# Tokens and first weights in one block, two more weight units fetched in the set-up, one power for sixteen columns

## The chip, the cores and the metric

The kernel runs on one core of a Trainium2 chip. The metric is the device time of one execution in microseconds (us). A core has TensorE (matrix products, with a weight load before each), VectorE, ScalarE, GpSimd and SyncE (SP), which here only issues DMAs. In the profile these are PE and PEld, DVE, ACT, POOL and SP; "SPq" is the issue of a DMA by SP, "ACTq" by ScalarE.

## What is computed

One layer of a decoder trunk on 512 tokens of 1024 channels, in float32. The change touches only its beginning:

```
h  = RMSNorm(x)                      # x: 512 x 1024
z  = h @ W_in                        # columns: retention q/k/v/gate, attention q/k/v of 3 groups, gates
aq = RMSNorm(aq per head); ak = RMSNorm(ak per head); rotary on both
x  = x + W_o( sig(g_A) * (retention @ W_A) + sig(g_B) * (attention @ W_B) )
x  = x + W_down( relu(RMSNorm(x) @ W_up)^2 )
x  = x + sig(RMSNorm(x) @ W_pg) * (p @ W_pp)
```

The attention has three groups of four heads of 128 channels. Each head's q and k are normed over their 128 channels.

## The kernel before

**Precision and tiling.** Each float32 product is made of three matmuls on parts: `hi` (rounded) and `lo` (the rest) of both operands, hi*hi, hi*lo, lo*hi (`mm3`, lines 249 to 251). Weights come from memory in units of 256 rows by 512 columns (`raw`, 512 KB, six buffers), and a unit is split into `whi` and `wlo` (`split_unit`, four buffers each): ScalarE writes `whi` (line 237), VectorE writes `wlo` (line 238). A panel of 512 output columns has 1024 rows, so four units. The plan's first three panels are the first group's queries (units 0 to 3), keys (4 to 7) and values (8 to 11).

**Order.** In the first group's query and key projections ScalarE and VectorE run in the order in which the program writes their instructions; the other queues are ordered by the planner, by readiness and place in the program. A queue runs its instructions one behind another, and one that waits holds what is behind it. `ahead(n)` splits units ahead of their use; `fetch(n)` issues the loads of the first n units of the plan, and a load waits for a free `raw` buffer.

**Set-up (`setup`).** ScalarE issues the gain columns (line 382). Then SP issues, for each of eight blocks of 128 rows, that block of the transposed `x` (line 388, from an array `x_cols`, 128 x 512) and that of the first panel's weights (line 391, from `w_in`, whose rows are 9728 long). Of the first weight block the first 64 rows are issued by ScalarE (line 393) and the rest by SP (line 394). Then come tables (lines 428, 432), `fetch(6)` (units 4 and 5, line 200) and the four tiles of `x` in rows (line 402). Seven matmuls on a constant run meanwhile (line 411).

**First panel (`first_panel`).** For each row block k, ScalarE and VectorE split `x` times the gain into `hh` and `hl` (lines 449, 450) and the weights into `whi` and `wlo`; the very first `whi` is a cast on VectorE (line 233). TensorE runs block 0 (lines 468 to 472), then blocks 1 to 3 for all four token tiles, then blocks 4 to 7 tile by tile, and hands each finished tile t to `consume` (line 586). That squares the four heads with a sum per head (ScalarE, line 591) and rotates the tile (VectorE, lines 544 to 549).

**The norms of the first panel.** The query projection of the first group is `lazy`: the factors of the token norm are not known until ScalarE has squared the four `x` tiles (`token_squares`, line 517) at the end of the panel. `token_factors` then makes them, with one power on GpSimd (line 527). Behind it, for each of the four tiles, `factor` makes a small VectorE instruction (line 613) and a power of 128x4 on GpSimd (line 614), and `scale` multiplies the rotated tile (VectorE, line 618). In VectorE's order the `wlo` of the key panel's units 6 and 7 follow the four scalings.

Of the kernel before, what the change touches and what calls it, by code (L numbers as in the profile page):

```python
# [11 lines left out]
F32 = mybir.dt.float32  # L12
F32R = mybir.dt.float32r
AF = mybir.ActivationFunctionType
ALU = mybir.AluOpType
AX = mybir.AxisListType

P = 128
S = 512
D = 1024  # L20
NT = S // P
KD = D // P
DFF = 4 * D
NF = DFF // 512
H = 4
HD = 128
# [9 lines left out]
AQ, AK, AV = 3072, 4608, 6144  # L36
# [40 lines left out]
class Block:  # L77
# [299 lines left out]
    def setup(self):  # L377
        nc, a = self.nc, self.a
        self.gcol = self.const.tile([P, 48], F32, name="gcol")
        xr = [self.big("xr") for _ in range(2)]  # L380
        self.x_cols = [xr[k // 4][:, k % 4] for k in range(KD)]
        nc.scalar.dma_start(self.gcol, a["vec_cols"])
        for u in range(KD // 2):
            src, _ = self.plan[u]
            raw = self.wraw.tile([P, 1024], F32, tag="raw", name=self.nm("raw")).rearrange("p (k n) -> p k n", k=2)
            for k in range(2):
                c = slice((2 * u + k) * P, (2 * u + k + 1) * P)
                nc.sync.dma_start(self.x_cols[2 * u + k], a["x_cols"][c])
                w = src[k * P : (k + 1) * P]
                if u or k:  # L390
                    nc.sync.dma_start(raw[:, k], w)
                else:
                    nc.scalar.dma_start(raw[: P // 2, k], w[: P // 2])
                    nc.sync.dma_start(raw[P // 2 :, k], w[P // 2 :])
            self.raws.append((raw, None))
        self.load_tables()
        self.fetch(6)
        self.x_tiles = []
        xb = [self.big("x") for _ in range(2)]
        for t in range(NT):  # L400
            v = xb[t // 2].rearrange("p (t c) n -> p t (c n)", t=2)[:, t % 2]
            nc.sync.dma_start(v, a["x"][0, t * P : (t + 1) * P])
            self.x_tiles.append(v)
        self.ident = self.const.tile([P, P], F32, name="ident")
        make_identity(nc, self.ident)
        warm = self.tmp("warm")
        nc.vector.memset(warm, 0.0)
        nc.scalar.activation(warm[:, 500:501], warm[:, 501:502], AF.Copy)
        wb, wps = warm.bitcast(mybir.dt.bfloat16), self.bank("warm")
        for _ in range(WARM):  # L410
            nc.tensor.matmul(wps, wb[:, :P], wb[:, :512], start=True, stop=True)
        self.mhalf = self.const.tile([P, H], F32, name="mhalf")
        nc.gpsimd.memset(self.mhalf, -0.5)
# [166 lines left out]
    def att_proj(self, g, n):  # L580
        nc = self.nc
        lazy = g == 0 and n == 0
        tabs = [] if lazy else [self.ready_tabs if g == 0 else self.tables(g, n)]
        rots, sums = [], []

        def consume(t, ps):
            ss, v, r = self.small(H, "ss"), self.small(H, "v"), self.small(H, "r")
            j = self.tmp("j")
            for h in range(H):
                c = slice(h * HD, (h + 1) * HD)  # L590
                nc.scalar.activation(j[:, c], ps[:, c], AF.Square, accum_out=ss[:, h : h + 1])
            C, Sn = tabs[0]
            rots.append(self.rotate(ps, C[:, t], Sn[:, t]))
            sums.append((ss, v, r))
            if not lazy:
                factor(t)
                if t:
                    scale(t - 1)
                if t == NT - 1:
                    scale(t)  # L600
            elif t == NT - 2:
                self.token_squares(0)
            elif t == NT - 1:
                self.token_squares(2)
                self.token_factors()
                for i in range(NT):
                    factor(i)
                for i in range(NT):
                    scale(i)

        def factor(t):
            ss, v, r = sums[t]
            nc.vector.tensor_scalar(v, ss, 1.0 / HD, self.floor[:, t : t + 1], op0=ALU.mult, op1=ALU.add)
            nc.gpsimd.tensor_tensor(r, v, self.mhalf[:, :H], op=ALU.pow)

        def scale(t):
            o = rots[t].rearrange("p (h e) -> p h e", h=H)
            nc.vector.tensor_tensor(o, o, sums[t][2].unsqueeze(2).to_broadcast([P, H, HD]), op=ALU.mult)

        if lazy:  # L620
            self.first_panel(consume, lambda: tabs.append(self.tables(g, n)))
        else:
            self.rows_gemm(self.hT, KD, consume)
        return self.heads_T(rots, g > 0, 16 if lazy else 12)
# [601 lines left out]
```

## Time and profile before

| | |
|---|---|
| median of 3 runs | 996.74 us (996.7 to 998.17) |
| the profiled execution | 997.21 us, its span 995.4 us |
| TensorE busy | 984.7 us, 4588 matmuls |
| VectorE busy | 647.6 us |
| ScalarE busy | 461.8 us |
| GpSimd busy | 97.4 us |
| moved by DMA | 141.15 MB, 142 GB/s on the mean |

The span runs from the first to the last instruction of the program in the profiled execution; its time is somewhat longer than the span. Times in the views below are counted from the span's start. A busy TensorE is one that has a matmul in its pipeline.

### The profile page before, as it was taken

The page shows a single profiled execution, that of the slowest core. Times are in us where ns is not written, and L with a number is a line of the kernel's source. Part 1 is how long each engine was busy: PE and PEld are TensorE (multiplying, and loading weights), DVE is VectorE, ACT ScalarE, POOL GpSimd, SP SyncE. Part 2 cuts the span into 40 slices and gives each one's busy share as a digit, 9 for nine tenths or more (in the row PEclk, how much of TensorE's full clock was granted, in tenths as well). Part 3 has the DMA queues.
Part 4 walks back from the last instruction along what each step waited for, and adds up shares of the span by engine and source line. Part 5 has one row for each costly group of instructions (what it writes and reads, how often), then busy time and mean ns, then how long its engine had stood idle before and what let it go on. Part 6 is the DMA issues. An engine that isn't in the chain of part 4 may idle for free.

```text
span 995.4 us, 12449 instructions
## 1 busy us (share of the span) xinstructions
PE 984.7 (99%) x4588; PEld 826.1 (83%) x4588; DVE 647.6 (65%) x1014; ACT 461.8 (46%) x938; POOL 97.4 (10%) x98
## 2 busy tenths in 40 slices
PE   8999999999999999999999999999999999999998
PEld 6788899889887888888888878888888888888886
DVE  6866675774878344554643696668667759766953
ACT  5535344433433334342422447764564565465451
POOL 0210220220000010001002010110101001000000
PEclk9999999999999999999999999999999999999999
DMA  9632132323353312222346496758659766875911
GB/s 337 240 101 76 54 106 85 105 76 106 93 142 120 113 43 85 86 85 85 132 146 166 125 233 193 190 128 225 179 136 212 203 167 153 238 160 131 312 54 53
DMA packets 90781, 141.15 MB, mean 142 GB/s; under 512 B 6320, under 2 KB 40416, under 8 KB 90720
## 3 DMA queue, kind: packets, MB, share of 16 engines
q1 hardware_dynamic: 79616, 119.22, 37.5%
q0 software_dynamic: 10880, 20.97, 12.7%
q8 instruction: 36, 0.59, 0.2%
q10 hardware_dynamic: 224, 0.16, 0.1%
q14 instruction: 25, 0.20, 0.1%
HBM read 136.10 MB, written 4.24 MB: 141 GB/s over the span
## 4 chain that ended last, share of the span: by engine, by line
PE 94%; DVE 4%; issue 1%; DMA 0%; ACT 0%; POOL 0%; ACTq 0%; DVEq 0%; POOLq 0%
PE pg L251 25%; PE pg L250 25%; PE pg L249 25%; PE pb L251 3%; PE pb L249 3%; PE pb L250 3%; PE po L700 1%; PE ph L559 1%; PE pt L325 1%; PE sc L677 1%; DVE wlo L238 1%; PE ry L899 1%; PE pe L651 1%; PE kv L887 1%; PE sc L683 1%
## 5 line engine op out<-in xcount | busy, mean ns | idle before, releaser
L238 DVE TENSOR_TENSOR wlo<-raw,whi 128x1024 fp32r<-128x1024 f32 (+1 forms) x166 | 196.8, 1191 | 103.8 <-ACT whi L237 101.8
L237 ACT ACTIVATE whi<-raw 128x1024 fp32r<-128x1024 f32 (+1 forms) x165 | 169.5, 1032 | 195.3 <-PE pg L251 75.4
L249 PE MATMUL pg<-whi,hh 128*128 128x512 f32 x444 | 178.6, 402 | 0.0
L250 PE MATMUL pg<-wlo,hh 128*128 128x512 f32 x444 | 173.6, 391 | 1.0 <-DVE wlo L238 1.0
L251 PE MATMUL pg<-whi,hl 128*128 128x512 f32 x444 | 173.7, 391 | 0.0
L250 PEld LDWEIGHTS pg<-wlo,hh 128*128 128x128 f32 x444 | 91.4, 206 | 15.3 <-DVE wlo L238 1.4
L251 PEld LDWEIGHTS pg<-whi,hl 128*128 128x128 f32 x444 | 91.1, 205 | 15.1
L249 PEld LDWEIGHTS pg<-whi,hh 128*128 128x128 f32 x444 | 91.3, 206 | 14.0
L249 PE MATMUL pg<-h2h,whi 128*128 128x512 f32 x256 | 99.6, 389 | 0.0
L250 PE MATMUL pg<-h2l,whi 128*128 128x512 f32 x256 | 99.6, 389 | 0.0
L251 PE MATMUL pg<-h2h,wlo 128*128 128x512 f32 x256 | 99.6, 389 | 0.0
L242 ACT ACTIVATE whi<-raw,gcol 128x256 fp32r<-128x256 f32 (+1 forms) x144 | 66.1, 523 | 21.3 <-PE pg L250 12.4
L243 DVE SCALAR_TENSOR_TENSOR wlo<-raw,gcol,whi 128x256 fp32r<-128x256 f32 (+1 forms) x144 | 65.5, 510 | 15.6 <-ACT whi L242 15.6
L202 POOL DMA_DIRECT2D raw<-in_w_down x32 | 38.6, 1206 | 302.4 <-DMA raw<-in_w_down 147.8
L249 PE MATMUL pg<-hh,whi 128*128 128x512 f32 x160 | 64.0, 400 | 0.0
L249 PE MATMUL pg<-whi,uh 128*128 128x512 f32 x160 | 62.8, 392 | 0.0
L251 PE MATMUL pg<-whi,ul 128*128 128x512 f32 x160 | 62.6, 392 | 0.0
L250 PE MATMUL pg<-wlo,uh 128*128 128x512 f32 x160 | 62.4, 390 | 0.0
L251 PE MATMUL pg<-hh,wlo 128*128 128x512 f32 x160 | 62.4, 390 | 0.0
L250 PE MATMUL pg<-hl,whi 128*128 128x512 f32 x160 | 62.3, 390 | 0.0
L250 PEld LDWEIGHTS pg<-h2l,whi 128*128 128x128 f32 x256 | 48.0, 188 | 10.0
L251 PEld LDWEIGHTS pg<-h2h,wlo 128*128 128x128 f32 x256 | 48.0, 188 | 10.0
(201 smaller groups left out, 1685.2 us busy)
## 6 DMA issues: line engine op xcount, KB each, us to landing
raw<-in_w_in SPq DMA_DIRECT2D x72, 512.0 KB, 4.1
raw<-in_w_down SPq DMA_DIRECT2D x48, 512.0 KB, 4.3
raw<-in_w_up SPq DMA_DIRECT2D x32, 512.0 KB, 5.2
raw<-in_w_down POOLq DMA_DIRECT2D x32, 512.0 KB, 6.7
raw<-in_w_o SPq DMA_DIRECT2D x12, 512.0 KB, 4.3
x<-in_x SPq DMA_DIRECT2D x8, 512.0 KB, 7.1
raw<-in_w_ret_out SPq DMA_DIRECT2D x8, 512.0 KB, 3.5
raw<-in_w_o POOLq DMA_DIRECT2D x8, 512.0 KB, 5.8
```

The costliest lines, as they stand in the source:

```text
L202: self.nc.gpsimd.dma_start(raw, rows(add[0]), accum_op=ALU.add)
L237: self.pin(nc.scalar.activation(R(hi[:, i]), raw[:, i], AF.Copy))
L238: nc.vector.tensor_tensor(R(lo[:, i]), raw[:, i], hi[:, i], op=ALU.subtract)
L242: self.pin(nc.scalar.activation(R(hi[:, i]), raw[:, i], AF.Copy, scale=g))
L243: nc.vector.scalar_tensor_tensor(R(lo[:, i]), raw[:, i], g, hi[:, i], op0=ALU.mult, op1=ALU.subtract)
L249: t.matmul(ps, sh, mh, start=first, stop=False, skip_group_check=more)
L250: t.matmul(ps, sh, ml, start=False, stop=False, skip_group_check=more)
L251: t.matmul(ps, sl, mh, start=False, stop=last, skip_group_check=more)
L325: nc.tensor.transpose(ps[:, k * P : (k + 1) * P], part[:, k * P : (k + 1) * P], self.ident)
L559: self.nc.tensor.transpose(ps[:, t * P : (t + 1) * P], rots[t][:, h * HD : (h + 1) * HD], self.ident)
L651: self.nc.tensor.transpose(ps[:, k * P : (k + 1) * P], e[:, k * P : (k + 1) * P], self.ident)
L677: nc.tensor.matmul(sc[:, h * P : (h + 1) * P], qT[:, h, rs], kT[:, h, rs], start=True, stop=True)
```

## The change

The transposed `x` and the first panel's weights are laid side by side on the host in one array `front` of 1024 x 1024: row r has the 512 tokens of channel r and then the 512 weights of row r. Each block of 128 rows is loaded by one DMA of 512 KB from SP, except block 0, whose `x` and weights are loaded by one DMA each; ScalarE issues none of them. The blocks lie in four of the 16 `big` buffers (two before), and the first panel takes no `raw` buffer. `fetch(8)` takes the place of `fetch(6)`, so that units 6 and 7 are issued before the `x` tiles. In the lazy projection the four powers of 128x4 become one of 128x16: the four small VectorE instructions write four columns each of one tile, one power reads all of it, and the four scalings follow.

```diff
@@ setup
         self.gcol = self.const.tile([P, 48], F32, name="gcol")
-        xr = [self.big("xr") for _ in range(2)]
-        self.x_cols = [xr[k // 4][:, k % 4] for k in range(KD)]
         nc.scalar.dma_start(self.gcol, a["vec_cols"])
+        self.x_cols = []
         for u in range(KD // 2):
-            src, _ = self.plan[u]
-            raw = self.wraw.tile([P, 1024], F32, tag="raw", name=self.nm("raw")).rearrange("p (k n) -> p k n", k=2)
+            front = self.big("front")
             for k in range(2):
-                c = slice((2 * u + k) * P, (2 * u + k + 1) * P)
-                nc.sync.dma_start(self.x_cols[2 * u + k], a["x_cols"][c])
-                w = src[k * P : (k + 1) * P]
-                if u or k:
-                    nc.sync.dma_start(raw[:, k], w)
-                else:
-                    nc.scalar.dma_start(raw[: P // 2, k], w[: P // 2])
-                    nc.sync.dma_start(raw[P // 2 :, k], w[P // 2 :])
-            self.raws.append((raw, None))
+                both = front[:, 2 * k : 2 * k + 2]
+                src = a["front"][(2 * u + k) * P : (2 * u + k + 1) * P].rearrange("p (c n) -> p c n", c=2)
+                for c in (0, 1) if u == 0 and k == 0 else (slice(0, 2),):
+                    nc.sync.dma_start(both[:, c], src[:, c])
+                self.x_cols.append(both[:, 0])
+            self.raws.append((front.rearrange("p (k c) n -> p k c n", c=2)[:, :, 1], None))
         self.load_tables()
-        self.fetch(6)
+        self.fetch(8)
@@ att_proj, consume
                 self.token_factors()
+                v4, r4 = self.small(NT * H, "v"), self.small(NT * H, "r")
                 for i in range(NT):
-                    factor(i)
+                    c = slice(i * H, (i + 1) * H)
+                    nc.vector.tensor_scalar(v4[:, c], sums[i][0], 1.0 / HD, self.floor[:, i : i + 1], op0=ALU.mult, op1=ALU.add)
+                    sums[i] = None, None, r4[:, c]
+                nc.gpsimd.tensor_tensor(r4, v4, self.mhalf.unsqueeze(1).to_broadcast([P, NT, H]), op=ALU.pow)
                 for i in range(NT):
                     scale(i)
@@ kernel
-    data["x_cols"] = np.ascontiguousarray(inputs["x"][0].T)
+    data["front"] = np.ascontiguousarray(np.concatenate(
+        [inputs["x"][0].T, inputs["w_in"][0][:, AQ : AQ + 512]], 1))
```

## Rows read from the trace of the kernel before

**Rows 1.** The page's first part: busy us, share of the span, instructions.

```profile
PE 984.7 (99%) x4588; PEld 826.1 (83%) x4588; DVE 647.6 (65%) x1014; ACT 461.8 (46%) x938; POOL 97.4 (10%) x98
```

**Rows 2.** Waits of TensorE over the span: us in total, times, longest.

```profile
PE pg L468 <- DVE whi L233: 1.9, 1, 1.9
...
PE ph L559 <- DVE ro L549: 1.2, 1, 1.2
PE pg L250 <- DVE wlo L238: 1.0, 1, 1.0
PE pc L756 <- DVE cw L754: 0.8, 1, 0.8
```

**Rows 3.** Timeline of the first 10 us: start, duration, engine, line, what [idle before].

```profile
1.18 0.55 SPq L394 DMA_DIRECT2D raw<-in_w_in  x1
...
3.96 0.72 ACT L449 ACTIVATE hh<-xr,gcol 128x512 fp32r<-128x512 f32 x1 [0.69 <-DMA gcol<-in_vec_cols]
...
5.96 0.43 DVE L233 CAST whi<-raw 128x512 fp32r<-128x512 f32 x1 [4.56 <-DMA raw<-in_w_in]
...
6.44 0.72 ACT L449 ACTIVATE hh<-xr,gcol 128x512 fp32r<-128x512 f32 x1 [1.76 <-DMA xr<-in_x_cols]
...
6.53 1.17 PE L468 MATMUL pg<-whi,hh 128*128 128x512 f32 x4 [1.90 <-DVE whi L233]
...
8.23 0.68 DVE L238 TENSOR_TENSOR wlo<-raw,whi 128x512 fp32r<-128x512 f32 x1
...
9.58 0.39 PE L250 MATMUL pg<-wlo,hh 128*128 128x512 f32 x1
```

**Rows 4.** DMA issues of the first 3 us: KB each, median us to landing.

```profile
raw<-in_w_in SPq DMA_DIRECT2D x1, 256.0 KB, 4.7
raw<-in_w_in SPq DMA_DIRECT2D x1, 128.0 KB, 3.1
```

**Rows 5.** Windows: length, busy by engine, granted clock, DMA share, GB/s.

```profile
6.50:9.40 2.90, 2.87 (x13) 2.41 (x14) 2.90 (x5) 2.52 (x5) 0.00 (x0) 1.00 1.03 372
```

**Rows 6.** Timeline: issue of the `x` tiles, and ScalarE's first and last square.

```profile
13.40 2.38 SPq L402 DMA_DIRECT2D x<-in_x  x4
...
27.25 1.11 ACT L517 ACTIVATE j<-x 128x1024 f32<-128x1024 f32 x1
...
31.72 1.06 ACT L517 ACTIVATE j<-x 128x1024 f32<-128x1024 f32 x1
```

**Rows 7.** The tile `x` in the first 40 us: its DMAs' landing.

```profile
DMA to landing us min/median/max: 8.3/9.2/11.1
```

**Rows 8.** The tile `raw` in the first 40 us: split times, waits for its DMAs.

```profile
L237 ACT ACTIVATE whi<-raw x15: 632/643/1061, 7.1 to 39.5; 128x512 fp32r<-128x512 f32 x11, 128x1024 fp32r<-128x1024 f32 x4
...
  DMA raw<-in_w_in: 4.6, 1
```

**Rows 9.** GpSimd's groups by shape: busy us, mean ns, idle before.

```profile
L614 POOL TENSOR_TENSOR r<-v,mhalf 128x4 f32<-128x4 f32 x24 | 29.9, 1251 | 156.4 <-DVE v L613 153.5 <-ACT whi L237 2.9
L315 POOL TENSOR_TENSOR r<-v,mhalf 128x1 f32<-128x1 f32 x16 | 8.7, 542 | 202.7 <-DVE v L314 202.7
L950 POOL TENSOR_TENSOR gm<-gt,gt 128x512 f32<-128x512 f32 x4 | 6.5, 1636 | 35.3 <-DVE gt L942 31.1 <-issue 4.2
```

**Rows 10.** Timelines of GpSimd, VectorE and TensorE from 34 to 41 us.

```profile
34.81 3.94 POOL L614 TENSOR_TENSOR r<-v,mhalf 128x4 f32<-128x4 f32 x4
...
35.86 0.69 DVE L618 TENSOR_TENSOR ro<-ro,r 128x512 f32<-128x512 f32 x1 [1.17 <-POOL r L614]
...
38.78 0.69 DVE L618 TENSOR_TENSOR ro<-ro,r 128x512 f32<-128x512 f32 x1 [0.28 <-POOL r L614]
39.39 4.62 DVE L238 TENSOR_TENSOR wlo<-raw,whi 128x1024 fp32r<-128x1024 f32 x4
...
39.27 0.39 PE L249 MATMUL pg<-whi,hh 128*128 128x512 f32 x1
40.66 0.50 PE L250 MATMUL pg<-wlo,hh 128*128 128x512 f32 x1 [1.00 <-DVE wlo L238]
```

## Prediction

> **What bounds the kernel now.** I read the page's first part before anything else: TensorE is busy for 984.7 of 995.4 us [rows 1]. Nothing in this change touches the number of its matmuls, so all that can be won or lost lies in the 10.7 us in which it is not busy. The list of TensorE's waits says where these are [rows 2]: 1.9 us before the first real matmul (line 468), 1.0 us at line 250 and two later ones of 1.2 and 0.8 us. The reader is to see that the list is short, and that two of its entries lie where the diff works.
>
> The first entry is opened by the timeline of the first 10 us [rows 3] with the landing times [rows 4]. The first weights' cast on VectorE waits 4.56 us for a DMA and starts at 5.96; the matmul follows at 6.53. The half of these weights that SP issued landed 3.1 us after its issue at 1.18, so at 4.3; what the cast waited for was the half on ScalarE's queue, at about 5.93. ScalarE had its own first input, the gain columns, at 3.96 and was through with `hh` at 4.7.
>
> The other entry lies at 39 us [rows 10]. The matmul at 39.27 is followed by the next at 40.66; the pace of this kernel is 0.22 us (13 matmuls in 2.87 us, [rows 5]), so 1.16 us are lost. It waits for `wlo` of the third weight unit of the key panel, and that stands on VectorE behind four scalings (line 618), each of which waits for its own power on GpSimd.
>
> **The block of memory (head).** Seventeen issues for eight row blocks become nine: `x` and weights of row block 0 by themselves on SP, then one of 512 KB for each later block. The bytes are the same, and the queue is full either way (372 GB/s from 6.5 to 9.4, [rows 5]), so fewer issues as such cost and save nothing; the DMA work hides them. The splits read views of the block with the same 128x512 shapes and cost what they cost. Four of the 16 big buffers are held where two were, until the panel's last split; no tile of this stretch needs the seventeenth. What moves is the first weights' second half: from ScalarE's queue to SP's, directly behind the first. 128 KB at 372 GB/s are 0.35 us, so the whole lands at 4.3 + 0.35 = 4.67 instead of 5.93. Bounds: 4.3 (as the first half now) and 5.93 (as now). From landing to first matmul it is 6.53 - 5.93 = 0.60 us; the new start is 5.27, or 1.26 us earlier.
>
> The next need is row block 1. Today its `x` lands by 6.44 (ScalarE's second `hh` starts then, released by it, [rows 3]) and its weights at 2.40 + 4.7 = 7.1 [rows 4]; with one transfer for both, `hh` must wait for the weights too. Call its landing T. Then `hh` takes 0.72, `whi` 0.64 [rows 8] and `wlo` 0.68 [rows 3]: the block's second matmul can go at T + 2.05. It goes at 9.58 today; with TensorE alone as the limit it would go at 5.27 + 3.05 = 8.32 (3.05 is today's distance from 6.53 to 9.58). For T I have two ends: 4.67 plus 512 KB at the full rate, 1.41 us, is 6.1; the weights' landing of today is 7.1. I take 6.5, nearer the low end, since 128 KB no longer compete from a second queue. That gives 8.55, a gain of **1.0 us**. T = 7.1 gives 9.15 and 0.45 us; first weights at 4.3 with T = 6.1 gives 8.15 and 1.4 us.
>
> A rule of the Trainium skill gives another figure: the page "DMA: Bandwidth & Descriptors" (section "Anatomy of one DMA — SWDGE (gpsimd) path") fits a DMA as about 2.0 us fixed plus its bytes at 436 GB/s, for GpSimd's path. By it, as an estimate, the first weights would land at 3.9, block 1 at 5.2, and the gain would be 1.8 us, so that the whole change came to nothing. The trace has 3.1 us for the landing of a half that the rule would put at 2.5 or so, so I stay with the rows.
>
> **Key weights ahead (`fetch(8)`).** Two more 512 KB loads stand on SP's queue ahead of the four `x` tiles. Who gains: nobody. In the first 40 us only one wait of an engine for weights is recorded, the 4.6 us at the start [rows 8]; the splits of the third and fourth key unit are held by the order of ScalarE and VectorE, not by their data. Who could lose: the `x` tiles, which come 1 MB later, 2.8 us at 372 GB/s. They are issued from 13.40 to 15.8 and land 8.3 to 11.1 us later, the first at 21.7, the last at about 26.6 [rows 6, 7]; behind the two loads that becomes 24.5 and 29.4. ScalarE squares the first at 27.25 and the last at 31.72 [rows 6]; with a head 1.0 us earlier that is 26.25 and 30.7. A margin of 1.3 us or more is left: cost 0 here. What is queued behind these squares, if the margin were gone, is the chain of the next part, so that a late tile costs its lateness in full.
>
> **One power for four tiles.** Removed: four powers of 128x4, 3.94 us together, 0.985 us each when they run one behind another. Added: one of 128x16. The trace has no such width. Nearest rows [rows 9]: a power of 128x1 takes 0.54 us, one of 128x4 1.25 us on the mean over the run (1.0 in this series). From one to four columns it grows, by 0.15 (to 1.0) to 0.24 us a column (to 1.25). So 16 columns take 0.54 + 15 x 0.15 = 2.8 at the least and 0.54 + 15 x 0.24 = 4.1 at the most by these, and 16/4 x 0.985 = 3.94 by the series itself. Costs of start that four instructions pay once each are already hidden in the series. I take 3.94, the row of the same place.
>
> What hangs on it is not GpSimd but the order behind it. Today the first scaling starts at 35.86, 1.05 us after the first power, and the other three run while later powers are worked; the last starts at 38.78 and `wlo` at 39.39 [rows 10], so a scaling costs VectorE 0.61 us. With one power no scaling can start before all 16 columns are there: 34.81 + 3.94 + 0.04 = 38.79. Four scalings, 2.44 us, put `wlo` at 41.23. That is **1.84 us later** than today. In general the shift is the power's duration less 2.10 us: 0.7 at 2.8 us, 2.0 at 4.1. TensorE is already waiting there, so the shift adds to its wait in full: 1.16 becomes 3.0 us. The four small VectorE instructions on the way (line 613) stay four, so nothing comes off there.
>
> **Sum.** Span 995.4 - 1.0 + 0 + 1.84 = 996.2. What follows is tied to TensorE's progress and moves with it: the later waits of 1.2 and 0.8 us are of VectorE's work on tiles that TensorE has just made. The profiled execution took 997.21 us, 1.81 around its span, so the same execution would take 998.0. It stood 0.47 us above the median of the three runs (996.74), so the median should be 997.5 us, 0.08% slower. Differences under 0.2% (2 us) can't be told from no change here, so this counts as the same.
>
> **Rivals.**
> *A power costs the same at any small width.* GpSimd's addition of 128x512 takes 1636 ns [rows 9], 3.2 ns a column; at such a price 16 columns take what 4 take, about 1.0 us. Then the scalings run from 35.86 on, `wlo` starts at 38.3, is done at 39.5, and the wait of 1.16 us is gone: 996.74 - 1.16 - 1.0 = 994.6. Against it stands the growth from one column to four. The page "GPSIMD Engine Reference" of the Trainium skill (section "Performance versus the Vector engine") has about 2.6 cycles an element for a two-input operation, which would lead here; the power's rows do not follow it. Chance 0.08.
> *The pair comes late.* If block 1 lands at 7.5 or the first weights at 5.9, the head gives nothing, and the median is 996.74 + 1.84 = 998.6, still within 0.2%. For it: the first transfers ran slowly (landings 3.1 us after 1.18, 4.7 us after 2.40). Against: the bytes ahead of both only become fewer. Chance 0.13.
> *The `x` tiles come late (slower).* They are now behind four weight units. Each us past 26.25 for the first, or 30.7 for the last, delays the squares, the powers and line 250 by one. It decides when the stall exceeds 1.2 us, the last tile landing after 31.9: with 1.5 us of stall the median would be 999.0. The 11.1 us of the slowest landing shows that a transfer can slip by 1 to 2 us, the margin is 1.3. Chance 0.07.
>
> **Chances and range.** My forecast has 0.70, the rivals 0.28, and 0.02 stays for anything else. Within the forecast the gain of 0.45 to 1.4 against the loss of 0.7 to 2.0 gives 996.0 to 998.3. The range of 8 in 10 takes in the late pair and part of the late tiles: 995.8 to 999.0. Faster by over 0.2% (below 994.75) needs the cheap power and the head's gain: 0.06. Slower by over 0.2% (above 998.73) needs late tiles, or a late pair with a power above 4.1 us: 0.10. The same: 0.84.
>
> **What the profile after would show.** The first real matmul near 5.3 and the second one of block 1 near 8.5. One power at line 606 or so of about 3.9 us, four scalings behind it without idle time between them, and a wait of TensorE at line 250 of 2.9 us where it was 1.0. No wait of ScalarE for `x`. A power near 1 us would make the forecast wrong towards faster, a recorded wait of ScalarE on `x` towards slower, and a first matmul still at 6.5 would shift it by one us.

## The result, and the profile after

The changed kernel takes 1001.52 us (median of 16 runs, 999.33 to 1003.45) against 998.25 us of the kernel before, timed beside it (16 runs, 996.47 to 1000.57): a ratio of 1.0031, 95% interval 1.0024 to 1.0039. That is slower, by 3.1 us; forecast were 0.8 us and no difference that can be told. The three runs shown ahead of the prediction (median 996.74) were at the lower end of the kernel's spread, for which the last experiments suggest a reason; put on that median, the ratio gives 999.8 us, which is outside the stated range too.

The profiled execution of the changed kernel has a span of 999.5 us, 4.1 more than before. The page's first part, beside [rows 1]:

```profile
PE 987.8 (99%) x4588; PEld 828.7 (83%) x4588; DVE 647.3 (65%) x1014; ACT 461.5 (46%) x938; POOL 96.4 (10%) x95
```

TensorE is busy for 3.1 us more, with as many matmuls, and not busy for 1.0 us more (11.7 where it was 10.7). So most of this loss does not lie in waits. TensorE's waits, beside [rows 2] (line 463 is 468 of before, 554 is 559, 755 is 756):

```profile
PE pg L250 <- DVE wlo L238: 2.5, 1, 2.5
...
PE ph L554 <- DVE ro L544: 1.2, 1, 1.2
PE pc L755 <- DVE cw L753: 1.0, 1, 1.0
PE pg L463 <- DVE whi L233: 0.8, 1, 0.8
```

The wait for the first weights shrank from 1.9 to 0.8 us; the one at line 250 grew from 1.0 to 2.5. What came of the first, in the timeline of the first 11 us, beside [rows 3] and, here first, two more matmul rows of before:

```profile
7.54 1.07 PE L470 MATMUL pg<-whi,hl 128*128 128x512 f32 x4
8.45 1.07 PE L472 MATMUL pg<-wlo,hh 128*128 128x512 f32 x4
```

And of the changed kernel:

```profile
4.81 0.43 DVE L233 CAST whi<-front 128x512 fp32r<-128x512 f32 x1 [3.41 <-DMA front<-in_front]
...
7.49 0.72 ACT L444 ACTIVATE hh<-front,gcol 128x512 fp32r<-128x512 f32 x1 [2.86 <-DMA front<-in_front]
...
5.38 2.05 PE L463 MATMUL pg<-whi,hh 128*128 128x512 f32 x4 [0.75 <-DVE whi L233]
7.23 1.91 PE L465 MATMUL pg<-whi,hl 128*128 128x512 f32 x4
8.94 1.16 PE L467 MATMUL pg<-wlo,hh 128*128 128x512 f32 x4
9.93 0.39 PE L249 MATMUL pg<-whi,hh 128*128 128x512 f32 x1
10.15 0.39 PE L250 MATMUL pg<-wlo,hh 128*128 128x512 f32 x1
```

TensorE starts at 5.38, as forecast (5.27), and still reaches the second matmul of row block 1 at 10.15 instead of 9.58. What took the gain here is the pace of the matmuls. The eight of lines 463 and 465 take 3.56 us (5.38 to 8.94), where the kernel before needed 1.92 (6.53 to 8.45): 0.43 us for each of line 465 and not 0.23, so they ran at the lower of TensorE's two clock levels (1.2 GHz).

The pair of block 1 landed only by 7.49 (I had 6.5), but in this execution that cost nothing: TensorE has no wait between 5.38 and 10.15. Where the clock is up early the late pair does hold it, as in the profile of e2 (the block alone, below), whose pair landed by 7.66:

```profile
7.66 0.72 ACT L444 ACTIVATE hh<-front,gcol 128x512 fp32r<-128x512 f32 x1 [3.12 <-DMA front<-in_front]
8.29 0.61 ACT L237 ACTIVATE whi<-front 128x512 fp32r<-128x512 f32 x1
...
7.21 1.07 PE L467 MATMUL pg<-wlo,hh 128*128 128x512 f32 x4
8.96 0.50 PE L249 MATMUL pg<-whi,hh 128*128 128x512 f32 x1 [0.68 <-ACT whi L237]
9.83 0.50 PE L250 MATMUL pg<-wlo,hh 128*128 128x512 f32 x1 [0.37 <-DVE wlo L238]
```

Either of the two is enough to undo the earlier start.

The stretch before line 250, by queue, beside [rows 10]:

```profile
33.26 0.69 DVE L568 TENSOR_TENSOR C<-rotc,mg 128x512 f32<-128x512 f32 x1 [0.61 <-DMA mg<-in_rot_gains]
...
36.09 2.90 POOL L606 TENSOR_TENSOR r<-v,mhalf 128x16 f32<-128x16 f32 x1
...
39.03 2.50 DVE L617 TENSOR_TENSOR ro<-ro,r 128x512 f32<-128x512 f32 x4 [3.07 <-POOL r L606]
41.45 4.62 DVE L238 TENSOR_TENSOR wlo<-raw,whi 128x1024 fp32r<-128x1024 f32 x4
...
39.85 0.39 PE L249 MATMUL pg<-whi,hh 128*128 128x512 f32 x1
42.72 0.50 PE L250 MATMUL pg<-wlo,hh 128*128 128x512 f32 x1 [2.48 <-DVE wlo L238]
```

The power takes 2.90 us and the four scalings follow it without idle time, as forecast in kind. New is the first row: VectorE waits for a DMA of `rot_gains`, the gains of the other groups' tables, which nothing in the diff names. And behind the gap, in windows (length; busy time of TensorE, its weight loads, VectorE, ScalarE and GpSimd; granted clock, DMA share, GB/s):

```profile
43.30:46.50 3.20, 3.20 (x9) 2.49 (x8) 2.77 (x3) 0.00 (x0) 0.00 (x0) 0.50 0.00 0
46.70:50.00 3.30, 3.30 (x16) 2.73 (x15) 1.67 (x4) 1.22 (x9) 0.00 (x0) 1.00 0.65 212
```

The granted clock is at half in the first window: 9 matmuls are started in its 3.2 us, 16 in the 3.3 us of the second. TensorE had just stood still for 2.5 us. Seven matmuls at 0.23 us are 1.6 us lost while TensorE counts as busy.

So the 4.1 us of this pair of profiles are: head +0.57; the late gains +0.7 (VectorE's chain is later by 1.28 at the first power, 36.09 - 34.81, of which 0.57 are the head); the power +0.8 (2.90 less 2.10, the prediction's own formula); the fall of the clock +1.6. About 0.4 is left, half of it at line 755, whose cause was not followed up.

### The profile page after: what moved, and what is told of

The parts are those of the page before. It is cut to its first block, busy times and chain, and to the rows that moved or that the text cites. A ratio compares the mean times of both kernels' runs of the same rounds, so it can differ in the third digit from the quotient of the medians.

```text
span 999.5 us, 12422 instructions
## 1 busy us (share of the span) xinstructions
PE 987.8 (99%) x4588; PEld 828.7 (83%) x4588; DVE 647.3 (65%) x1014; ACT 461.5 (46%) x938; POOL 96.4 (10%) x95
## 4 chain that ended last, share of the span: by engine, by line
PE 92%; DVE 4%; DMA 3%; POOL 0%; issue 0%; SPq 0%; ACT 0%; DVEq 0%; ACTq 0%; POOLq 0%
PE pg L251 25%; PE pg L249 25%; PE pg L250 25%; PE pb L251 3%; PE pb L250 3%; PE pb L249 3%; PE po L699 1%; PE ph L554 1%; DMA raw<-in_w_in 1%; DMA mg<-in_rot_gains 1%; PE pt L325 1%; DMA front<-in_front 1%; PE sc L676 1%; PE ry L898 1%; PE pe L650 1%; PE kv L886 1%
## 5 line engine op out<-in xcount | busy, mean ns | idle before, releaser
L238 DVE TENSOR_TENSOR wlo<-raw,whi 128x1024 fp32r<-128x1024 f32 (+1 forms) x158 | 191.2, 1215 | 102.2 <-ACT whi L237 100.2
L237 ACT ACTIVATE whi<-raw 128x1024 fp32r<-128x1024 f32 (+1 forms) x158 | 165.0, 1049 | 193.6 <-PE pg L251 75.9
L249 PEld LDWEIGHTS pg<-h2h,whi 128*128 128x128 f32 x256 | 48.1, 188 | 9.9
```

What stands on the lines that cost most here:

```text
L237: self.pin(nc.scalar.activation(R(hi[:, i]), raw[:, i], AF.Copy))
L238: nc.vector.tensor_tensor(R(lo[:, i]), raw[:, i], hi[:, i], op=ALU.subtract)
L249: t.matmul(ps, sh, mh, start=first, stop=False, skip_group_check=more)
```

## The experiments

All were timed against the kernel before on the same chip. The ratio is not the quotient of the two medians, so the two can differ (e3 is 1.1 us slower by the ratio and 0.4 by the medians); the text goes by the ratio and its interval unless it says otherwise. "Wait" is TensorE's longest wait at line 250 in the one profile of each kernel; "low" counts the executions whose mean granted clock was 0.998 or less, which is what about 3.4 us at half clock amount to. A clock that is low at the start does not show in that mean: f7's profile has a mean of 1.0, though its matmuls of line 465 ran at 0.43 us.

| kernel | median us | ratio to before (95%) | wait us | low |
|---|---|---|---|---|
| before (beside e1 to e4; beside f1 and f3 to f5; beside f2, f6, f7 and g1) | 998.04, 998.55, 998.66 | 1 | 1.0 | 10 of 96 |
| changed | 1001.52 | 1.0031 (1.0024 to 1.0039) | 2.5 | 12 of 16 |
| e1 one power alone | 1000.47 | 1.0022 (1.0013 to 1.0030) | 1.8 | 7 of 11 |
| e2 block alone | 999.92 | 1.0018 (1.0008 to 1.0027) | 2.1 | 9 of 12 |
| e3 block and fetch(8) | 998.40 | 1.0011 (1.0001 to 1.0020) | 2.8 | 5 of 12 |
| e4 changed, one split first | 999.43 | 1.0023 (1.0013 to 1.0033) | 2.2 | 4 of 12 |
| f1 before, two splits first | 997.70 | 0.9993 (0.9985 to 1.0002) | none | 2 of 11 |
| f3 changed, two splits first, gains early | 996.62 | 0.9987 (0.9978 to 0.9996) | none | 1 of 11 |
| f4 block alone, two DMAs a block | 1000.05 | 1.0017 (1.0008 to 1.0026) | 2.7 | 7 of 11 |
| f5 changed, gains early | 999.09 | 1.0012 (1.0003 to 1.0021) | 1.8 | 3 of 11 |
| f2 before, 11 warm matmuls | 997.45 | 0.9990 (0.9980 to 0.9999) | 1.0 | 0 of 11 |
| f6 before, two splits first, 11 warm | 995.96 | 0.9973 (0.9962 to 0.9985) | none | 0 of 6 |
| f7 block alone, gains early | 998.16 | 0.9990 (0.9981 to 0.9999) | 1.0 | 0 of 11 |
| g1 as f3, 9 warm | 996.64 | 0.9980 (0.9971 to 0.9989) | none at the key units | 1 of 11 |

**e1, the power alone.** The kernel before with the last hunk of `consume` from the diff, nothing else.

> The kernel before with the one power of 128x16 alone. My theory: the power takes 2.9 us as in the changed kernel, the third key unit's split starts 0.8 us later than before (40.2 instead of 39.4), TensorE's gap at line 250 grows from 1.39 to about 2.2 us and the time by 0.8 us (0.08%), plus up to 1.7 us in the executions in which the granted clock falls to its lower level behind the gap. Rival 1 (the power is harmless, the block and the fetch are the cause): gap and time as before, within 0.3 us. Rival 2 (the clock falls whenever the gap is over 2 us): time plus 2.5 us.

```profile
36.64 2.90 POOL L611 TENSOR_TENSOR r<-v,mhalf 128x16 f32<-128x16 f32 x1
...
11.42 0.39 PE L250 MATMUL pg<-wlo,hh 128*128 128x512 f32 x1
```

The power took 2.90 us, the wait grew from 1.0 to 1.8 us. The first rival fell. The time grew by 2.2 us (1.3 to 3.0), more than the 0.8 of the wait, and the fall of the clock does not account for the rest: the profiled execution had no fall behind its gap, and the seven executions with a low mean (999.10 to 1001.38) were no slower than the four others (999.83 to 1001.07). The profile's own span is 2.6 us longer than that of before because it reaches the second matmul of row block 1 at 11.42 instead of 9.58, with a clock that rose late, and because of the 0.8. Why the median of e1 is higher by more than the 0.8 stays open.

**e2 and e3, the block without and with `fetch(8)`.** Both are the changed kernel with four powers as before.

```diff
@@ setup                    # e2 only
-        self.fetch(8)
+        self.fetch(6)
@@ att_proj, consume        # shortened: "..." stands for the lines of the one power
-                v4, r4 = self.small(NT * H, "v"), self.small(NT * H, "r")
                 for i in range(NT):
-                    ...
+                    factor(i)
```

> The block alone: fetch(6) and four powers as before. My theory: the first real matmul starts at 5.4 us, row block 1 lands near 7.5, so that its second matmul goes at 9.6 to 10.2 us (9.58 before) and the block gives nothing: 0 to 0.6 us slower, gap at line 250 as before (1.4 us). Which of the two ends comes from the clock of the first matmuls: at its lower level until 9 us, or at its higher one from 5 us. Rival (the block brings the 1.0 us that I predicted and the loss is all elsewhere): the second matmul of block 1 at 8.6 us and the time 1.0 us shorter.

> The changed kernel with four powers as before, so the block and fetch(8). My theory: the gains of the other two groups land at 33.2 us instead of 29.9, VectorE waits 0.6 us for them before the norm factors, the gap at line 250 is about 2.0 us (1.4 before), and the time is 0.7 us above that of the block alone. Rival 1 (fetch(8) costs nothing): no wait of VectorE for these gains, gap 1.4 us. Rival 2 (the clock of the stretch behind the gap is what costs): its granted clock falls here in as many executions as in the changed kernel, and the time is 2 us or more above the block alone.

In e2 the gap did not stay as it was, and that was the most telling miss. The late gains are there without `fetch(8)` (VectorE's rows of e2):

```profile
33.48 0.69 DVE L568 TENSOR_TENSOR C<-rotc,mg 128x512 f32<-128x512 f32 x1 [0.99 <-DMA mg<-in_rot_gains]
...
40.89 4.62 DVE L238 TENSOR_TENSOR wlo<-raw,whi 128x1024 fp32r<-128x1024 f32 x4
```

So it is the block that makes them late. Units 0 to 3 no longer take `raw` buffers; loads of units 6 to 9, which used to wait for one, are ready at once and stand on SP ahead of the gains. SP's rows of before and of the changed kernel (the issue at line 432, or 427, is that of the gains):

```profile
17.71 0.38 SPq L200 DMA_DIRECT2D raw<-in_w_in  x1
19.13 0.33 SPq L432 DMA_DIRECT2D mg<-in_rot_gains  x1
20.53 1.65 SPq L200 DMA_DIRECT2D raw<-in_w_in  x2
```

```profile
13.89 4.35 SPq L397 DMA_DIRECT2D x<-in_x  x4
19.27 1.73 SPq L200 DMA_DIRECT2D raw<-in_w_in  x2
21.98 0.34 SPq L431 DMA_DIRECT2D mg<-in_c_mask  x1
23.33 0.34 SPq L427 DMA_DIRECT2D mg<-in_rot_gains  x1
```

The gains go out at 23.33 instead of 19.13. With `fetch(8)` as well (e3), VectorE's wait for them was longer in the one profile, which was the slowest execution of e3, and TensorE's 2.8 us instead of 2.1:

```profile
35.09 0.69 DVE L568 TENSOR_TENSOR C<-rotc,mg 128x512 f32<-128x512 f32 x1 [1.73 <-DMA mg<-in_rot_gains]
```

That `fetch(8)` costs 0.7 us over the block alone was not seen in the times: e3 is no slower than e2 (their intervals overlap).

**f5 and f7, the gains early.** The changed kernel (f5) and the block alone (f7), each with the second load of gains behind the `x` tiles:

```diff
@@ setup, behind the loop over the x tiles
+        self.gain_rows(1, NG)
@@ load_rest
-        self.gain_rows(1, NG)
```

> The changed kernel, with the other groups' gains loaded behind the x tiles, ahead of units 8 and 9, instead of behind them. My theory (the block frees four raw buffers, so loads of weights that used to wait for a buffer go ahead of the gains on SP): the gains land near 30 us, VectorE does not wait for them, the gap at line 250 shrinks from 2.9 us by 0.6 to 1.0, and the clock falls in fewer executions: 0.7 to 2 us under the changed kernel. Rival (only the power makes the gap): gap and time unchanged within 0.3 us.

> The block alone (fetch(6), four powers) with the other groups' gains loaded behind the x tiles. My theory: with the gains in time, VectorE does not wait for them and the gap at line 250 is that of the kernel before, 1.4 us, so that only the block's effect on the head is left: median within 0.7 us of the kernel before, 1 to 1.5 us under the block alone. Rival (the block loses by its late second row block, not by the gains): 1 us or more above the kernel before, gap of 1.4 us all the same.

The waits of TensorE, f5 first and then f7:

```profile
PE pg L250 <- DVE wlo L238: 1.8, 1, 1.8
```

```profile
PE pg L250 <- DVE wlo L238: 1.0, 1, 1.0
```

Both waits came out as the theory had it. In f7 the wait at line 250 is 1.0 us again, and no execution of 11 has the low mean; in f5 it is 1.8, that of the power alone. The changed kernel's 3.1 us became 1.2 in f5. The block with its gains in time is 2.8 us under the block alone by the ratios (I had 1 to 1.5), and the low means are gone with the wait. It is little faster than the kernel before: 1.0 us by the ratio (0.1 to 1.9), 0.5 by the medians. Where it comes from is not shown. It is not the head as I had it: f7's own profile has the clock low until about 10 us, and reaches the second matmul of block 1 at 10.75,

```profile
5.62 2.05 PE L463 MATMUL pg<-whi,hh 128*128 128x512 f32 x4 [0.99 <-DVE whi L233]
...
10.75 0.40 PE L250 MATMUL pg<-wlo,hh 128*128 128x512 f32 x1
```

where e1, which has the set-up of before and a low clock too, reaches it at 11.42. That an early start is worth something to executions with a late clock is what these two profiles suggest, no more.

**f4, the block in two DMAs.** As e2, with `for c in (0, 1):` for every row block.

> The block alone (fetch(6), four powers), but x and weights of every row block by a DMA each, as block 0 has it. My theory (the pair holds back hh, since one transfer lands as a whole): x of block 1 lands near 6.5 us and its weights near 7.2, hh and whi follow each by itself, and the second matmul of block 1 can go at 9.2 or earlier instead of 9.8 to 10.2 where the clock is up by then: 0.6 us under the block alone. Rival (the bytes of the first blocks come late whatever the pieces): x of block 1 lands no earlier than 7.3, nothing gained.

```profile
5.25 0.72 ACT L444 ACTIVATE hh<-front,gcol 128x512 fp32r<-128x512 f32 x1 [0.57 <-DMA front<-in_front]
7.02 0.63 ACT L237 ACTIVATE whi<-front 128x512 fp32r<-128x512 f32 x1 [1.05 <-DMA front<-in_front]
```

`hh` of block 1 starts at 5.25 where e2 has 7.66, `whi` at 7.02 where e2 has 8.29: the one transfer does hold `hh` back, and the rival fell. No time was gained over e2; the profiled execution had the clock low until the block was done, and the gap at line 250 is there as in e2. For the time this one is inconclusive.

**e4 and f3, the gap taken out of the changed kernel.** `self.ahead(n)` splits key units ahead of the scalings in VectorE's order:

```diff
                 nc.gpsimd.tensor_tensor(r4, v4, ..., op=ALU.pow)
+                self.ahead(3)        # e4; self.ahead(4) in f3, with the early gains of f5
                 for i in range(NT):
                     scale(i)
```

> The changed kernel, whole, with one more thing: the third key unit's split stands ahead of the four scalings in VectorE's order. My theory: the power and the late gains delay only VectorE, which now has the split behind it already; no gap at line 250, so 2.6 us of waiting are gone, and with the gap the fall of the clock behind it (1.7 us): 4.3 us faster than the changed kernel where that falls, 2.6 where it does not, so 0.5 us under the kernel before or about equal to it. Rival (the clock falls for another reason, the late start of TensorE): the gap goes, the fall at 43 us stays, and the time is 2.6 us under the changed kernel, 1.5 above the kernel before.

> The changed kernel with both splits ahead of the scalings and the other groups' gains loaded behind the x tiles, ahead of further weights. My theory: no gap at line 250, no wait of VectorE for the gains, and so no fall of the clock at 42 to 47 us in any execution; of the change's loss only the head is left, 0 to 0.6 us, and the gap that the kernel before has (1.16 us) is gone too: 0 to 1 us under the kernel before, 3 to 4 under the changed one. Rival (the head is most of the loss): 1 us or more above the kernel before even so.

e4 missed: with one split ahead, the next unit's split waited behind the scalings, and TensorE stood for 2.2 us one unit later:

```profile
43.91 0.50 PE L250 MATMUL pg<-wlo,hh 128*128 128x512 f32 x1 [2.16 <-DVE wlo L238]
```

With two (f3) it does not wait at all at the key units:

```profile
33.77 4.90 POOL L606 TENSOR_TENSOR r<-v,mhalf 128x16 f32<-128x16 f32 x1
...
33.55 2.35 DVE L238 TENSOR_TENSOR wlo<-raw,whi 128x1024 fp32r<-128x1024 f32 x2
38.71 2.50 DVE L618 TENSOR_TENSOR ro<-ro,r 128x512 f32<-128x512 f32 x4 [2.80 <-POOL r L606]
```

f3 is faster than the kernel before, by 1.3 us (0.4 to 2.2). But it has two edits that the change has not, and one of them, the splits first, gives 0.7 us to the kernel before by itself (f1, -0.2 to 1.5). That the change as such is worth anything once its gap is gone is not shown. In the profiled execution of f3, the fastest of its eleven, the pair of block 1 was in time and the clock was up, and the second matmul of block 1 went at 8.48; the prediction had 8.55.

**f1, f2, f6 and g1: the kernel before without its wait, and the clock at the start.** f1 is the kernel before with `self.ahead(4)` ahead of its scalings; f2 has `WARM = 11`; f6 both; g1 is f3 with `WARM = 9`.

> The kernel before, with the splits of the third and fourth key units ahead of the four scalings in VectorE's order, under the four powers. My theory (TensorE's gap at line 250 is VectorE's order alone): the gap of 1.4 us is gone, 1.16 us are saved, no fall of the clock behind it in any execution: 1 to 1.5 us (0.1 to 0.15%) under the kernel before. Rival (VectorE's work beside GpSimd's powers slows these, and the scalings come too late for the transposes of the queries): the gap goes but a wait of about the same length shows up at the transposes (line 559), time unchanged.

> The kernel before with 11 matmuls on the constant in place of 7, so TensorE works from 1.5 to about 6.2 us and the first real matmul follows at 6.5. My theory: what varies from execution to execution of one kernel by 2 us (996 to 998.5) is whether the granted clock is up at the first real matmul; it rises near 5 us in some profiles and near 10 us in others, after an idle stretch of 1.9 us behind the seventh matmul. Without the idle stretch it is up by 7 us in every execution: median 996.7, 1 to 1.5 us under the kernel before. Rival (the rise has nothing to do with the idle stretch): late rises stay, median unchanged within 0.5 us.

> The kernel before with both splits ahead of the scalings and 11 warm matmuls. My theory: both gains add, 1.2 us for the gap and 1 to 1.5 us for the early clock, median near 996, 2.3 us under the kernel before. Rival (only one of the two is worth anything): 1 us under it.

> The changed kernel with both splits ahead of the scalings, early gains (as in f3) and 9 warm matmuls instead of 7, which end at 5.3 us, where the first real matmul starts. My theory: the clock is up at the first matmul or soon after in every execution, which f3 has in about half of them: 0.5 to 1 us under f3, near 995.8, 2.5 us under the kernel before. Rival (the clock rises late as often as before): as f3, 996.6.

f1 took the wait away and shows no new one at the transposes, so its rival fell; its 0.7 us can't be told from nothing. f2's executions lie between 996.19 and 997.82 with one at 999.24, those of the kernel before beside it between 996.20 and 1000.56: so the spread of the kernel before seems to be mostly the clock at the start. f6 is the best kernel here, 2.7 us (1.5 to 3.8) under the one before, and its six executions lie within 1.1 us. g1 came out as its rival had it: its median is f3's.

## Why the prediction was wrong

**Right.** That the two places are the head and line 250. That scalings can't start before the whole power is done, and that the shift adds to TensorE's wait in full: 1.8 us of wait in e1 where 1.0 + 0.8 was due by the formula. The start of TensorE (5.38 for 5.27). That the `x` tiles are not late: ScalarE never waited for them.

**The first step that failed: "Key weights ahead", "cost 0 here", with only the `x` tiles named as what could be late.** The paragraph on the block counts the `big` buffers that it takes and not the `raw` buffers that it gives back. I counted what the loads are moved past by `fetch`, and not what the block releases: four `raw` buffers, and with them loads that go ahead of every later issue of SP. The transfer that became late was the other groups' gains. I had not looked for VectorE instructions of a later group in this stretch; `tables` of group 1 (line 573) stand among the norms, and VectorE holds everything behind them. Late gains are 0.7 us of TensorE's wait in the profile, and f5 takes 1.9 us of the change's 3.1 away.

**The second step that failed: "all that can be won or lost lies in the 10.7 us in which it is not busy".** TensorE can lose time while it counts as busy, and 3.1 of the 4.1 us of the two profiles were lost so. The clock had no term. A wait of 2 to 3 us was priced at its length, and the matmuls of row block 0 at the pace of the one profile that I had. In the changed kernel's profile the wait was followed by about 3.4 us at half clock, 1.6 us more; profiles of e2, e3, f4 and f5 show such a stretch behind their gap too, those of e1 and e4 do not. Low means stand in 47 of 85 executions of the seven kernels with a wait of 1.8 us or more, and in 14 of 157 of those with 1.0 us or none. In six of the seven, every execution with a low mean is slower than every one without; in the changed kernel it is 1000.80 to 1003.45 for twelve and 999.33 to 999.71 for four. On the means the two sorts are 1.4 to 2.4 us apart, at times more than the 1.6 us of such a stretch, so they may differ in more than the clock. e1 is the exception. The changed kernel's four are 1.4 us over the mean of the kernel before; the rest of its loss goes with the low mean.

That the longer wait brings the fall is what this points to, since the low means are gone with the wait in f3 (1 of 11) and in f7, which has the 1.0 us of before (0 of 11); for a single execution it isn't certain, as the profiles of e1 and e4 show.

**Terms mis-sized.** The power: 2.90 us and not 3.94, so the shift was 0.8 and not 1.84; my lower bound, 0.54 + 15 x 0.15 = 2.8, was right, and the series that I preferred had a start of its own in each of its four powers (three starts fewer for 1.04 us less, so about 0.35 us each, an estimate). The landing of block 1: 7.5 in the profile after, 6.2 to 8.0 over the profiles with one transfer, where I had 6.1 to 7.1. Why it varies is open. It lands late enough to cost the gain of the head, as in e2, but in the profile after it was the clock that took it.

The two errors of size partly cancelled by luck (head +1.6 in the profile, power -1.0); the wrong verdict came from the late gains and the clock, neither of which had a term or a rival. The "slower" rival named the right kind of thing, a transfer pushed back on SP's queue, and the wrong transfer.

## What to carry to other kernels

When an edit gives buffers back, ask which waiting loads that sets free, where they stand on the DMA queue, and what every engine next needs from what is now behind them; look for instructions of later stages that the planner has placed early. One instruction in place of several makes the first consumer wait for the last element: if the consumers ran under the producer, work without that need must be moved between them, as the two splits were in f3 and f6. A wait of TensorE can cost more than its length, since the clock may be low behind it while TensorE counts as busy: 1.6 us behind the 2.5 us wait of the changed kernel's profile. The idle stretch ahead of the first real matmul is such a place too: to fill most of it and to remove the wait at line 250 was worth 2.7 us (1.5 to 3.8) in f6.

## What the runs showed of the hardware

**The clock at the start.** With the same seven warm matmuls the rise came anywhere from about 4 to over 10 us after the span's start, by the pace of the matmuls in the profiles: in f7 line 465 still ran at 0.43 us from 7.5 us on, in f3 line 463 ran near 0.23 from 5.4 on. The profile's granted clock reads 1.0 in these first us at either pace. The Trainium skill (page "TensorE: Matmul & The Clock Gate", section "Part 1: The HAM clock gate") says that the point of rise varies from run to run of one kernel. These traces agree: the kernel before, f1 and e1 have one set-up, and line 249 begins row block 1 at 9.35, 10.33 and 11.19 us. With the idle stretch filled (f2) ten of eleven executions lie within 1.7 us, where those of the kernel before spread over 4.4.

**GpSimd's power beside VectorE's splits.** The power of 128x16 took 2.90 us with VectorE idle (e1, f5 and the changed kernel) and 4.90 us with two splits beside it (f3); with one it took 3.76 (e4). The Trainium skill (page "GPSIMD Engine Reference", section "Key points") says that GpSimd shares its interfaces to the on-chip memory (SBUF) with VectorE and that instructions of VectorE with two inputs from there contend with it. The splits are such instructions, and this is what it cost. The widths give 0.54, 1.0 and 2.90 us for 1, 4 and 16 columns.
